# A transformer-like block on one core: cross queries and six of eight convolution columns by seven half-size products, computed ahead of the heads, with results through DRAM

## The chip, the core and the metric

The kernel runs on one core of one Trainium2 chip. A core has TensorE (PE, matrix products; its weight loads are a track of their own, PEld), VectorE (DVE), ScalarE (ACT), GpSimd (POOL) and SyncE (SP, which here only issues DMAs). TensorE writes its results to PSUM, and VectorE and ScalarE read them from there. Each engine works through its own instructions in a fixed order and waits at semaphores for the others. The metric is the device time of one execution in microseconds; less is better.

## What is computed

One layer for 1024 tokens of 1024 channels, in float32, and 256 memory tokens. Cut to what matters:

```python
h = rms_norm(x, g_mix)
c_h, c_b, c_c, sq, sk, sv, xq, gate_pre = split(h @ w_in)     # 1024 columns each, gates 3072
y_conv = (c_b * causal_depthwise_conv(c_c * c_h, conv_w)) @ w_conv_out     # width 3
y_sb   = stick_breaking_attention(sq, sk, sv) @ w_sb_out                   # 16 heads of 64
y_x    = memory_cross_attention(xq, rms_norm(mem), w_mem_kv, ...) @ w_x_out  # 4 heads of 256
g      = sigmoid(gate_pre)
x = x + (g0 * y_conv + g1 * y_sb + g2 * y_x) @ w_out
h2 = rms_norm(x, g_mlp)
x = x + square(relu(h2 @ w_up)) @ w_down
```

Each head of the cross attention normalises its queries and keys, so the queries need a sum of squares over 256 channels.

## The kernel before

**Precision.** Every operand of a matrix product is held as two parts, high and low, each in a reduced format; ScalarE rounds the high part and VectorE subtracts it from the source for the low one (split_w, split; L88 to L118). A product of two such operands is three matmuls: high by high, high by low, low by high (mm3, mm3_steps). A weight tile of 128 x 1024 is loaded by SP into one of 4 buffers (rawp) and split into one of 3 double buffers (whlp) or into two pages. A page is 128 x 1024 floats of SBUF; there are 40, and nearly everything lives in them. The Tile framework gives buffers out, sets the waits and may move an instruction ahead of others on its engine; where the code says keep_in_program_order, the instructions so marked stay in written order among themselves.

**A column of w_in** means 128 of its output channels. project_steps (L211) computes one for 512 tokens: 8 k-tiles by 3 matmuls of 128 x 128 by 128 x 512, 24 in all, yielding twice, so that it can be used as filler: 12 matmuls a step.

**The order of the work.**
1. The start (L316 to L382): memory rows are normalised and transposed; kv(0) to kv(7) compute keys and values in eight groups of 48 matmuls with 256 columns (L281); x is normalised and transposed in two halves into the sixteen pages of hT (norm_transpose, L172, split on the way); the queries of cross head 0 (xq_half, L236), whose squares ScalarE takes from PSUM, and the transposed keys (k_transpose, L357) are woven in.
2. The cross heads (L471 to L493): for each head scores, softmax, transposes and values for two halves of the tokens. Between them run filler steps: for heads 0 to 2 eight steps of the next head's queries, for head 3 the first steps of the values for the other attention (v_steps, L445). Then the rest of the values, whose results go to DRAM, and queries and keys of head pair 0 (sb_qk, L498).
3. The attention heads (L676 to L721): eight pairs, eight query blocks each for two heads. TensorE's scores, ScalarE's sigmoids, POOL's masks, VectorE's scan and product, transposes, splits and the values, two and three steps behind. Filler steps are the gates' columns, the next pair's sb_qk, and in the last pair convolution column 0.
4. Convolution columns 1 to 7 (L722, conv_steps at L625): three products per column, their product with the three taps by ScalarE and VectorE (L644, L646), results split into pages. After that the outputs of the three branches are multiplied by their matrices and gates and merged (L730 to L753), and w_out follows.
5. The MLP's up-projection (L892 to L1036) already uses seven products: the product of a 2 x 2 block matrix by a 2 x 2 block matrix (two columns by two halves of k; two halves of k by two halves of the tokens) needs seven half-size products instead of eight. The operands are sums and differences of blocks (S1 to S4 of the weights, T1 to T4 of the activations, h2_second_a and h2_second_b), and the partial results are accumulated in two PSUM banks and a few SBUF tiles. One unit of two columns is 7 x 12 = 84 matmuls where the plain way takes 96. The order of one unit's products is p1, p2, p6, p5, p7, p3, p4; p1, p6, p7 and p4 accumulate in one bank, and ScalarE copies the state of that bank out after p1 and after p6. All of its vector work is kept in written order.
6. The down-projection, in the same way, and the output.

Of the kernel before, what the change touches and what calls it, by code (L numbers as in the profile page):

```python
# [16 lines left out]
P = 128  # L17
# [25 lines left out]
def block_kernel(ctx, tc, x, mem, small, w_in, w_v, w_kv, w_co, w_so, w_xo, w_out, w_up, w_dn, out):  # L43
# [118 lines left out]
    hT = [None] * KT  # L162

# [47 lines left out]
    def project_steps(w, th, done, cuts=2):  # L211

        ps = pd()
        yield from mm3_steps(
            ps, [(cut(w, k * P, (k + 1) * P), cut(hT[k], th * 512, th * 512 + 512)) for k in range(KT)], cuts
        )
        done(ps)
# [8 lines left out]
    def x_dst(th):  # L226
        def dst(k):
            if hT[k] is None:
                hT[k] = (page(), page())
            return cut(hT[k], th * 512, th * 512 + 512)  # L230

        return dst

    xq_w = {}

    def xq_half(h, st, d2, th, cuts=2):  # L236

        if th == 0:
            if (h, d2) not in xq_w:
                xq_w[h, d2] = unit(w_in[CT_XQ + 2 * h + d2])  # L240
            st["q"][d2] = (page(), page())
            st["sq"][d2] = page(F32)

        def done(ps):
            s = slice(th * 512, th * 512 + 512)
            nc.scalar.activation(st["sq"][d2][:, s], ps, AF.Square)
            q = st["q"][d2]
            split(ps, q[0][:, s], q[1][:, s], scale=sm[:, C_GQ + d2 : C_GQ + d2 + 1])
            if d2 == 1:
                sq = st["sq"]  # L250
                nc.gpsimd.tensor_tensor(out=sq[0][:, s], in0=sq[0][:, s], in1=sq[1][:, s], op=ALU.add)

        yield from project_steps(xq_w[h, d2], th, done, cuts)

    def xq_scale(st):

        sq = st["sq"]
        pss = pt()
        for t in range(8):
            nc.tensor.matmul(  # L260
                pss[:, t : t + 1], lhsT=sq[0][:, t * P : (t + 1) * P], rhs=ones, start=True, stop=True
            )
        r = rstd(pss[:, 0:8], 8, 256)
        st["sc"], st["nsc"] = stat(8), stat(8)
        nc.vector.tensor_scalar_mul(st["sc"], r, 1.0 / 16.0)
        nc.vector.tensor_scalar_mul(st["nsc"], r, -1.0 / 16.0)

    def xq_new():
        return {"q": [None, None], "sq": [None, None]}
# [6 lines left out]
    def kv_split(cg):  # L276
        if cg not in kv_w:
            kv_load(cg)
        kv_w[cg] = [halves(r, True) for r in kv_w[cg]]

    def kv(cg):  # L281

        us = kv_w.pop(cg)
        for i in range(NM):
# [10 lines left out]
            if cg < 4:  # L295
                nc.scalar.copy(kn[i][:, c0 : c0 + 256], ps)
            else:
                split(ps, vx[i][0][:, c0 : c0 + 256], vx[i][1][:, c0 : c0 + 256])

    def k_norm(i):  # L300
# [10 lines left out]
        for h in range(NXH):  # L311
            nc.vector.tensor_scalar_mul(
                kn[i][:, h * 256 : h * 256 + 256], kn[i][:, h * 256 : h * 256 + 256], r[:, h : h + 1]
            )

# [13 lines left out]
    rows0 = [normed(t) for t in xrows]  # L329
    run(kv(1))  # L330
    xq_raw = [load(w_in[CT_XQ + d2]) for d2 in range(2)]
    xrows = load_rows(x, 512, 4)
    kv_split(2)
    kv2 = kv(2)
    for k, _ in enumerate(norm_transpose(rows0, x_dst(0), C_GMIX)):
        fill(kv2, 1)
        if k in (2, 5):
            xq_w[0, k // 3] = halves(xq_raw[k // 3])
    run(kv2)
    st0 = xq_new()  # L340
    run(xq_half(0, st0, 0, 0))
    kv_split(3)
    rows1 = [normed(t) for t in xrows]
    run(xq_half(0, st0, 1, 0))
    kv_split(4)
    weave(norm_transpose(rows1, x_dst(1), C_GMIX), kv(3))
    vx = [(page(), page()) for _ in range(NM)]
    kv_split(5)
    run(kv(4))
    for i in range(NM):  # L350
        k_norm(i)
    run(xq_half(0, st0, 0, 1))
    kv_split(6)
    run(kv(5))
    kx_t = [(page(), page()) for _ in range(2)]

# [16 lines left out]
    def kx(h, d2):  # L373
        dt_ = 2 * h + d2
        return cut(kx_t[dt_ // 4], (dt_ % 4) * M, (dt_ % 4 + 1) * M)

    weave(k_transpose(), xq_half(0, st0, 1, 1, 8))
    kv_split(7)
    run(kv(6))
    xq_scale(st0)  # L380
    run(kv(7))
    pin[0] = False  # L382


    o_scr = [
        [dram.tile([P, 1024], F32, name=f"oscr_{b}_{k}") for k in range(KT)] for b in range(2)
    ]
    g_scr = [
        [dram.tile([P, 1024], F32, name=f"gscr_{b}_{k}") for k in range(KT)] for b in range(3)
    ]  # L390
    v_scr = [dram.tile([P, 4, 1024], F32, name=f"vscr_{c}") for c in range(2)]

# [52 lines left out]
    def v_steps():  # L445

        us = [unit(w_v[0, kp], True) for kp in range(4)]
        for cg in range(2):
            un = []
            for j in range(8):  # L450
                if cg == 0 and j >= 4:
# [6 lines left out]
                            cut(hT[k], j * P, (j + 1) * P),  # L458
# [11 lines left out]

    vgen = v_steps()  # L471
    for h in range(NXH):
        if h + 1 < NXH:
            st1 = xq_new()
            more = chain(*(xq_half(h + 1, st1, d2, th) for d2 in range(2) for th in range(2)))
        else:
            st1, more = None, vgen
        p0 = x_scores(h, st0, 0)
        fill(more, 2)
        p1 = x_scores(h, st0, 1)  # L480
        fill(more, 2)
# [6 lines left out]
        if st1:  # L488
            run(more)
            xq_scale(st1)  # L490
# [272 lines left out]
    }  # L763

# [406 lines left out]
```

## Time and profile before

| | |
|---|---|
| median of 3 runs | 2244.83 us (2242.71 to 2245.02) |
| profiled execution, its own time | 2243.7 us |
| its span in the profile | 2242.0 us |
| TensorE busy | 2187.6 us, 98% of the span, 10304 matmuls |
| VectorE, ScalarE, POOL busy | 58%, 42%, 16% |
| mean granted TensorE clock | 0.994 |
| moved by DMA | 241.91 MB, mean 108 GB/s |

The profile's times are microseconds from the start of the span. A row of the windows gives, for a stretch of the span, its length and the busy time and number of instructions of PE, PEld, DVE, ACT and POOL, then the granted TensorE clock (1 is full speed), the DMA engines' busy share and GB/s. A row of the timeline gives start, duration, engine, line of the code, operation, output and input by the program's names (d, z, t and o are PSUM banks, pg a page, whl a split weight, raw a loaded one), shapes, a count where alike instructions are merged, and in brackets how long the engine sat idle before it and what ended that. A row of the groups gives busy time, the mean ns of one instruction and the idle time before.

### The profile page before, as it was taken

The page shows a single profiled execution, that of the slowest core. Times are in us where ns is not written, and L with a number is a line of the kernel's source. Part 1 is how long each engine was busy: PE and PEld are TensorE (multiplying, and loading weights), DVE is VectorE, ACT ScalarE, POOL GpSimd, SP SyncE. Part 2 cuts the span into 40 slices and gives each one's busy share as a digit, 9 for nine tenths or more (in the row PEclk, how much of TensorE's full clock was granted, in tenths as well). Part 3 has the DMA queues.
Part 4 walks back from the last instruction along what each step waited for, and adds up shares of the span by engine and source line. Part 5 has one row for each costly group of instructions (what it writes and reads, how often), then busy time and mean ns, then how long its engine had stood idle before and what let it go on. Part 6 is the DMA issues. An engine that isn't in the chain of part 4 may idle for free.

```text
span 2242.0 us, 27020 instructions
## 1 busy us (share of the span) xinstructions
PE 2187.6 (98%) x10304; PEld 1817.1 (81%) x10304; DVE 1310.4 (58%) x1781; ACT 948.3 (42%) x1726; POOL 367.4 (16%) x550
## 2 busy tenths in 40 slices
PE   7999999999999999999999999999889999999999
PEld 7988888878878878888888888888678888788887
DVE  5633218787787787773332334442565655777776
ACT  6544316565565665652221121121555555433332
POOL 1011103333333333320000000000111222100000
PEclk9999999999999999999999999999899999999999
DMA  6311322122222222211111344233134444754444
GB/s 226 104 57 59 122 74 85 66 79 82 68 82 77 72 79 76 76 48 57 48 48 47 122 150 150 96 138 114 52 127 155 155 155 150 271 174 141 141 153 139
DMA packets 68786, 241.91 MB, mean 108 GB/s; under 512 B 9008, under 2 KB 9008, under 8 KB 68656
## 3 DMA queue, kind: packets, MB, share of 16 engines
q1 hardware_dynamic: 50224, 177.26, 24.5%
q0 software_dynamic: 18432, 62.93, 7.6%
q8 instruction: 81, 1.33, 0.3%
q14 instruction: 49, 0.40, 0.1%
HBM read 168.85 MB, written 62.91 MB: 103 GB/s over the span
## 4 chain that ended last, share of the span: by engine, by line
PE 80%; DVE 7%; ACT 4%; issue 4%; POOL 3%; DMA 0%; POOLq 0%; DVEq 0%; ACTq 0%; SPq 0%
PE d L205 12%; PE d L207 12%; PE d L206 12%; PE d L810 4%; PE d L806 4%; PE d L125 4%; PE d L127 4%; PE d L809 4%; PE d L126 4%; PE z L806 3%; PE z L809 3%; PE z L810 3%; POOL pg L558 2%; PE o L597 2%; DVE pg L114 1%
## 5 line engine op out<-in xcount | busy, mean ns | idle before, releaser
L205 PE MATMUL d<-pg,whl 128*128 128x512 f32 x1152 | 456.4, 396 | 0.0
L207 PE MATMUL d<-pg,whl 128*128 128x512 f32 x1152 | 449.9, 390 | 0.0
L206 PE MATMUL d<-pg,whl 128*128 128x512 f32 x1152 | 449.7, 390 | 0.0
L777 ACT ACTIVATE pg<-pg 128x512 f32<-128x512 f32 (+2 forms) x180 | 140.2, 782 | 295.9 <-DVE pg L774 293.9
L207 PEld LDWEIGHTS d<-pg,whl 128*128 128x128 f32 x1152 | 216.2, 188 | 47.0
L205 PEld LDWEIGHTS d<-pg,whl 128*128 128x128 f32 x1152 | 216.5, 188 | 40.9
L206 PEld LDWEIGHTS d<-pg,whl 128*128 128x128 f32 x1152 | 216.6, 188 | 40.5
L558 POOL TENSOR_SCALAR_AFFINE_SELECT pg<-pg 128x128 f32<-128x128 f32 x256 | 168.0, 663 | 304.8 <-ACT pg L555 291.8
L568 DVE TENSOR_TENSOR_SCAN pg<-pg,zero 128x128 f32<-128x128 f32 (+7 forms) x128 | 177.3, 1385 | 57.5 <-POOL pg L558 55.0
L90 DVE TENSOR_TENSOR whl<-raw,whl 128x1024 fp32r<-128x1024 f32 x96 | 121.7, 1268 | 152.4 <-ACT whl L89 151.6
L113 ACT CAST pg<-t 128x256 fp32r<-128x256 f32 (+2 forms) x336 | 115.2, 368 | 203.9 <-DVE pg L114 141.5
L89 ACT CAST whl<-raw 128x1024 fp32r<-128x1024 f32 x96 | 101.5, 1058 | 228.4 <-PE d L207 82.6
L774 DVE TENSOR_TENSOR pg<-pg,pg 128x1024 fp32r<-128x1024 f32 (+3 forms) x144 | 149.6, 1043 | 64.4 <-ACT pg L777 63.1
L114 DVE TENSOR_TENSOR pg<-t,pg 128x256 fp32r<-128x256 f32 (+2 forms) x336 | 129.3, 404 | 65.6 <-ACT pg L113 62.1
L125 PE MATMUL d<-pg,whl 128*128 128x512 f32 x384 | 149.4, 389 | 0.0
L126 PE MATMUL d<-pg,whl 128*128 128x512 f32 x384 | 149.4, 389 | 0.0
L127 PE MATMUL d<-pg,whl 128*128 128x512 f32 x384 | 149.4, 389 | 0.0
L205 PE MATMUL d<-pg,pg 128*128 128x512 f32 (+1 forms) x384 | 138.9, 362 | 0.4 <-ACT pg L116 0.4
L206 PE MATMUL d<-pg,pg 128*128 128x512 f32 (+1 forms) x384 | 137.9, 360 | 0.5 <-DVE pg L90 0.5
L207 PE MATMUL d<-pg,pg 128*128 128x512 f32 (+1 forms) x384 | 137.9, 360 | 0.0
L806 PE MATMUL d<-pg,whl 128*128 128x512 f32 x288 | 115.3, 401 | 11.8 <-ACT whl L777 7.7
L809 PE MATMUL d<-pg,whl 128*128 128x512 f32 x288 | 114.8, 398 | 1.2 <-DVE pg L774 1.2
(180 smaller groups left out, 4176.3 us busy)
## 6 DMA issues: line engine op xcount, KB each, us to landing
raw<-in_w_in SPq DMA_DIRECT2D x72, 512.0 KB, 3.6
raw<-in_w_up SPq DMA_DIRECT2D x32, 512.0 KB, 4.0
raw<-fscr_s SPq DMA_DIRECT2D x32, 512.0 KB, 4.0
pg<-in_w_dn SPq DMA_DIRECT2D x32, 512.0 KB, 5.1
gscr<-pg POOLq DMA_DIRECT2D x24, 512.0 KB, 2.9
raw<-gscr SPq DMA_DIRECT2D x24, 512.0 KB, 3.3
fscr<-pg POOLq DMA_DIRECT2D x48, 256.0 KB, 3.3
fscr_s<-pg POOLq DMA_DIRECT2D x48, 256.0 KB, 2.9
```

The source lines that it names most:

```text
L114: nc.vector.tensor_tensor(out=lo, in0=src, in1=f32v(hi), op=ALU.subtract)
L125: nc.tensor.matmul(ps, lhsT=ah, rhs=bh, start=i == 0, stop=False)
L126: nc.tensor.matmul(ps, lhsT=ah, rhs=bl, start=False, stop=False)
L127: nc.tensor.matmul(ps, lhsT=al, rhs=bh, start=False, stop=i == n - 1)
L205: nc.tensor.matmul(ps, lhsT=ah, rhs=bh, start=i == 0, stop=False)
L206: nc.tensor.matmul(ps, lhsT=ah, rhs=bl, start=False, stop=False)
L207: nc.tensor.matmul(ps, lhsT=al, rhs=bh, start=False, stop=i == n - 1)
L558: nc.gpsimd.affine_select(out=t_[:, W - P : W], in_=t_[:, W - P : W], pattern=[[-1, P]], compare_op=ALU.is_gt, fill=fill_, base=0, channel ...
L568: nc.vector.tensor_tensor_scan(out=rev, data0=rev, data1=zero.broadcast_to([P, W]), initial=1.0, op0=ALU.mult, op1=ALU.add)
L806: m_ = nc.tensor.matmul(ps, lhsT=ah, rhs=bh, start=first and i == 0, stop=False, **go)
L809: nc.tensor.matmul(ps, lhsT=ah, rhs=bl, start=False, stop=False, **go)
L810: nc.tensor.matmul(ps, lhsT=al, rhs=bh, start=False, stop=i == n - 1, **go)
```

## The change

The seven-product unit is made general and used twice more. Seconds holds the activations' halves and their sums and differences for a normalised x, Unit the seven products of one pair of columns, drive the order of a list of units (the old order of the MLP's units, with the list extra put between the first products). Four units make the cross queries (one per head); nine make convolution columns 2 to 7: for each pair of columns one unit for the h part, one for the C part, one for the B part. They run right after the start and before the cross heads. Their results go to DRAM by POOL's queue: raw queries to q_scr, finished convolution columns to u_scr. Column 0 stays filler of the last head pair, column 1 becomes filler of the cross heads, together with sb_qk of pair 0.

```diff
+    class Seconds:
...
+        def first(self, rows):
+            for kk in range(4):
+                raw = self.raw[kk] = pair()
+                for j in range(2):
+                    self.tile(rows, kk + 4 * j, raw[:, j, :])
+                    yield
+                hi, lo = pair(F32R), pair(F32R)
+                split(flat(raw), flat(hi), flat(lo))
...
+        def second_a(self, rows, kk):
+
+            r0, r1, ta = self.raw[kk], pair(), pair()
+            for j in range(2):
+                self.tile(rows, kk + 4 * j, r1[:, j, :])
+            if self.keep:
+                nc.gpsimd.dma_start(out=self.keep[kk // 2][:, kk % 2, :], in_=r1[:, 0, :])
+            vec(ta[:, 0, :], r1[:, 0, :], ALU.subtract, r0[:, 0, :])
+            vec(ta[:, 1, :], r1[:, 1, :], ALU.subtract, ta[:, 0, :])
+            self.h["t1"][kk], self.h["t2"][kk] = split_pair(ta)
+            vec(r0[:, 0, :], r1[:, 1, :], ALU.subtract, r1[:, 0, :])
+            vec(r0[:, 1, :], r0[:, 1, :], ALU.subtract, ta[:, 1, :])
+            self.new[kk] = r1
...
+            if u < 2:
+                un.w4()
+            else:
+                un.p1()
+                U[u - 1].fin()
+                un.w3()
+                un.p2()
+                un.w4()
+            if u + 2 < NU:
+                U[u + 2].load()
+            if u >= 2:
+                un.p6()
+                un.p5()
+            if u >= 1 and nx:
+                nx.w1()
+            un.p7()
+            if u == 0:
+                nx.w3()
+            elif nx:
+                nx.w2()
+            un.p3()
+            un.p4()
```

The first stages in their new order. kv's results for the values and the normalised keys go to DRAM and come back later; the queries and the key transposes leave this stage:

```diff
+    weave(sec_h.first(rows0), kv(2))
     kv_split(3)
+    kv_load(4)
     rows1 = [normed(t) for t in xrows]
...
+    run(kv(3))
+    kv_load(5)
     for i in range(NM):
         k_norm(i)
...
+    for kk in range(4):
+        kv_split(4 + kk)
+        steps = kv(4 + kk)
+        fill(steps, 4)
+        if kk + 6 < 8:
+            kv_load(kk + 6)
+        sec_h.second_a(rows1, kk)
+        run(steps)
+    for i in range(NM):
+        nc.gpsimd.dma_start(out=kv_scr[1][i], in_=vr[i])
```

The new units. fin of a unit is called in the unit after it, behind that one's p1; act and vec keep the written order, and so do the taps here:

```diff
+    class CUnit(Unit):
...
+        def fin(self):
+            self.cv = []
+            for i in range(2):
+                prod = flat(self.tiles[i])
+                vec(prod, prod, ALU.mult, flat(self.hu.tiles[i]))
+                cv = flat(self.hu.tiles[i])
+                taps(self.c0 + i, prod, cv, act, lambda **kw: order(nc.vector.scalar_tensor_tensor(**kw)))
+                self.cv.append(cv)
...
+    class BUnit(Unit):
...
+        def fin(self):
+            for i in range(2):
+                b = flat(self.tiles[i])
+                vec(b, b, ALU.mult, self.cu.cv[i])
+                nc.gpsimd.dma_start(out=u_scr[self.c0 + i], in_=b)
...
+    units = [QUnit(h) for h in range(NXH)]
+    for c in range(2, KT, 2):
+        hu = HUnit(c)
+        cu = CUnit(c, hu)
+        units += [hu, cu, BUnit(c, cu)]
+    drive(units, [lambda kk=kk: sec_h.second_b(kk) for kk in range(4)])
+
+
+    h12 = [load(t.rearrange("p a b -> p (a b)")) for t in h12_scr]
+    kn = [page(F32) for _ in range(NM)]
+    for i in range(NM):
+        nc.sync.dma_start(out=kn[i], in_=kv_scr[0][i])
+    for kk in range(4):
...
+        split_o(h12[kk // 2][:, j * 512 : j * 512 + 512], *sec_h.h["12"][kk])
```

The values and the cross heads. Queries are loaded, squared and split from SBUF (xq_load, xq_split), and a head has five filler steps of 12 matmuls:

```diff
+    vgen = v_steps()
+    fill(vgen, 17)
+    st0 = xq_load(0)
+    vr = [load(kv_scr[1][i]) for i in range(NM)]
+    weave(k_transpose(), vgen)
+    vx = [halves(r, True) for r in vr]
+    xq_split(st0)
+    more = chain(sb_qk(0, nxt), conv_steps(1))
+    fill(more, 1)
+    xq_scale(st0)
+    st1 = None
+    for h in range(NXH):
+        if h + 1 < NXH:
+            st1 = xq_load(h + 1)
+        p0 = x_scores(h, st0, 0)
+        fill(more, 1)
+        p1 = x_scores(h, st0, 1)
+        fill(more, 1)
+        t0 = x_transpose(p0)
+        fill(more, 1)
+        x_values(h, 0, t0)
+        if h + 1 < NXH:
+            xq_split(st1)
+        fill(more, 1)
+        t1 = x_transpose(p1)
+        fill(more, 1)
+        if h + 1 < NXH:
+            xq_scale(st1)
+        x_values(h, 1, t1)
+        st0 = st1
+    run(more)
```

In the last pair the finished columns come back, and the loop over columns 1 to 7 is gone:

```diff
+                if p == NPAIR - 1 and hd == 1 and i in (3, 5, 6, 7):
+                    u.append(unit(u_scr[1 + len(u)], True))
...
+    while len(u) < KT - 1:
+        u.append(unit(u_scr[1 + len(u)], True))
     run(more)
-    for c in range(1, KT):
-        run(conv_steps(c))
+    u = u0 + u
```

The MLP's units become a subclass of Unit with the same instructions in the same order.

546 lines of the change are left out of this document (253 added, 293 removed).

## The prediction

> **What bounds the kernel now.** I read the page first: engine totals, the chain that ended last, the groups.
>
> ```profile
> PE 2187.6 (98%) x10304; PEld 1817.1 (81%) x10304; DVE 1310.4 (58%) x1781; ACT 948.3 (42%) x1726; POOL 367.4 (16%) x550
> PE 80%; DVE 7%; ACT 4%; issue 4%; POOL 3%; DMA 0%; POOLq 0%; DVEq 0%; ACTq 0%; SPq 0%
> L205 PE MATMUL d<-pg,whl 128*128 128x512 f32 x1152 | 456.4, 396 | 0.0
> ```
>
> TensorE is busy nearly always and carries 80% of the chain. So a removed matmul counts, but its price is not the 396 ns of its row. In the timeline of TensorE the starts show the price:
>
> ```profile
> 20.04 0.28 PE L207 MATMUL d<-pg,pg 128*128 128x256 f32 x1
> 20.16 0.28 PE L205 MATMUL d<-pg,pg 128*128 128x256 f32 x1
> 1652.23 0.39 PE L806 MATMUL d<-pg,whl 128*128 128x512 f32 x1
> 1652.46 0.39 PE L809 MATMUL d<-pg,whl 128*128 128x512 f32 x1
> 1607.56 1.03 PE L819 MATMUL t<-ident,pg 128*128 128x128 f32 x8
> 1608.35 0.48 PE L806 MATMUL d<-pg,whl 128*128 128x512 f32 x1
> ```
>
> Busy times overlap: a 512-column matmul starts 0.23 us after the last one, a 256-column one 0.12 us, eight transposes take 0.79 us. Now the windows, cut where the stages end:
>
> ```profile
> 0.00:100.70 100.70, 87.79 (x592) 80.27 (x593) 60.48 (x100) 61.95 (x113) 12.46 (x21) 0.98 0.53 183
> 100.70:240.00 139.30, 138.46 (x756) 119.28 (x755) 51.76 (x125) 58.06 (x130) 23.77 (x26) 1.00 0.16 57
> 240.00:334.20 94.20, 94.17 (x416) 77.66 (x415) 14.14 (x15) 19.63 (x29) 10.36 (x15) 1.00 0.32 101
> 334.20:1011.40 677.20, 659.95 (x3242) 545.32 (x3242) 530.50 (x760) 400.15 (x935) 246.02 (x350) 1.00 0.23 74
> 1011.40:1240.00 228.60, 228.60 (x1011) 189.28 (x1010) 72.29 (x78) 45.53 (x57) 1.30 (x2) 1.00 0.15 49
> 1680.00:1736.00 56.00, 56.00 (x249) 46.37 (x248) 33.68 (x45) 29.61 (x44) 11.27 (x21) 1.00 0.47 155
> ```
>
> They are: the start (memory keys and values, normalised x, head 0's queries); the cross heads; the rest of the values and pair 0; the attention heads; the conv columns 1 to 7; a stretch of the MLP's up-projection, which already uses seven products. The conv stage is 7 x 144 = 1008 matmuls in 228.6 us, 0.2268 us each with no gap. The up stretch is as dense, so a seven-product unit in full swing costs its matmuls alone: 84 x 0.2268 = 19.05 us, where the plain way takes 96.
>
> **Part 1, products.** Removed: 8 query columns (384 matmuls) and 6 conv columns (864), 1248 in all, 283.0 us. Added: 13 units of 84, 1092, 247.7 us. Gain 35.4 us. The group's mean of 390 to 396 ns would have made it 61. [...]
>
> Everything after 1240.0 us is the same work in the same order, so I forecast the new time of that mark, stage by stage.
>
> **Part 2, the start.** Its present 100.7 us hold 384 kv matmuls (46.1 us), 96 query matmuls (21.8) and 96 transposes (9.5): 77 us of work, 23 of loss. Up to 26.6 us nothing changes. The queries and the key transposes leave, and with them TensorE's cover for the vector work; the second half's tiles get differences and splits (second_a) instead of one split. Its rows, from the MLP's entry, and those of splits:
>
> ```profile
> 26.64 1.13 PE L178 MATMUL t<-ident,pg 128*128 128x128 f32 x6
> 1600.67 1.48 DVE L774 TENSOR_TENSOR pg<-pg,pg 128x512 f32<-128x512 f32 x2
> 1603.28 1.23 DVE L774 TENSOR_TENSOR pg<-pg,pg 128x1024 fp32r<-128x1024 f32 x1 [1.12 <-ACT pg L777]
> 1605.02 2.08 DVE L774 TENSOR_TENSOR pg<-pg,pg 128x512 f32<-128x512 f32 x3
> 1608.23 1.23 DVE L774 TENSOR_TENSOR pg<-pg,pg 128x1024 fp32r<-128x1024 f32 x1 [1.12 <-ACT pg L777]
> 27.11 2.00 ACT L89 CAST pg<-raw 128x1024 fp32r<-128x1024 f32 x2
> 68.41 2.35 DVE L90 TENSOR_TENSOR pg<-raw,pg 128x1024 fp32r<-128x1024 f32 x2
> ```
>
> One second_a holds VectorE for 1608.23 - 1603.28 = 4.95 us, its own wait for ScalarE included; a kv group's two splits add 2.3. Four rounds make 29 us, against 4 x (5.8 + 0.8) = 26 us on TensorE: VectorE paces this loop. It begins after first() with kv(2), paced by ScalarE (from 29.1 us eight tile copies of 0.6, four splits of 1.0 and evictions: about 39) and after kv(3) (5.8 us and a wait for its split: 46), with the norms of rows 4 to 7 and the key norms in the way of ScalarE: at 47 to 50. The loop then ends at 76 to 79. I take **79**, the late end, since a gap of 2 to 4 us ahead of kv(4) may halve the clock once. Bounds: 71 (TensorE's own work from 39) and 86 (two half-clock spells and 2 us more).
>
> **Part 3, the units.** The prologue has second_b alone. Up to w2 of unit 1, VectorE has two w1 (2.4 us), four second_b (1.9 each), two sums (0.7) and two w2 (3.6 each, rows below): about 18 us, some of it ahead of the first product, where TensorE has six products, 16 us: 1 us lost (0 to 5). Q and H units are lighter than the up units (no relu, no sums). The C units are not. Their fin (product and taps, all in written order) is issued in the B unit that follows, between p1's copy and w3. Rows for it:
>
> ```profile
> 1604.14 0.60 ACT L777 ACTIVATE xh<-d 128x512 f32<-128x512 f32 x1 [0.90 <-PE d L810]
> 998.83 1.15 ACT L644 ACTIVATE pg<-pg,sm 128x1024 f32<-128x1024 f32 x1 [1.65 <-DVE pg L637]
> 1000.78 2.59 DVE L646 SCALAR_TENSOR_TENSOR pg<-pg,sm,pg 128x1023 f32<-128x1023 f32 x2
> 1654.32 1.22 DVE L774 TENSOR_TENSOR whl<-raw,whl 128x1024 fp32r<-128x1024 f32 x1
> 1636.65 0.69 DVE L774 TENSOR_TENSOR pg<-raw,raw 128x512 f32<-128x512 f32 x1
> 1637.97 1.06 ACT L777 ACTIVATE whl<-pg 128x1024 fp32r<-128x1024 f32 x1 [2.10 <-DVE pg L774]
> 1639.06 1.22 DVE L774 TENSOR_TENSOR whl<-pg,whl 128x1024 fp32r<-128x1024 f32 x1 [1.12 <-ACT whl L777]
> ```
>
> Clock from the start of B's p1. p1 ends at 2.9; ScalarE copies it to 3.5, and only then may start the first tap, to 4.6. VectorE adds two taps to 7.2, then multiplies the second column (1.2) to 8.3; ScalarE's second tap to 9.5; two more on VectorE to 12.1. Now w3: two subtractions to 13.3, ScalarE's high part to 14.4, w4's high part to 14.9, and behind it in ScalarE's order the copy of p6, to 15.5. p7 continues in p6's bank and needs that copy, and w3's weights. TensorE is there after p1, p2, p6, p5 = 48 x 0.2268 = 10.9 us. So it waits **4.6 us** in each of three B units. What such a wait does to the clock:
>
> ```profile
> 1598.54 0.69 PE L819 MATMUL t<-ident,pg 128*128 128x128 f32 x2 [3.99 <-DVE pg L159]
> 1600.74 0.63 PE L809 MATMUL d<-pg,whl 128*128 128x512 f32 x1
> 1601.16 0.63 PE L810 MATMUL d<-pg,whl 128*128 128x512 f32 x1
> 1603.71 0.39 PE L810 MATMUL d<-pg,whl 128*128 128x512 f32 x1
> 1622.64 0.79 PE L806 MATMUL d<-pg,whl 128*128 128x512 f32 x1 [2.96 <-ACT pg L777]
> 1627.78 0.40 PE L809 MATMUL z<-pg,whl 128*128 128x512 f32 x1
> 1639.08 0.80 PE L806 MATMUL d<-pg,whl 128*128 128x512 f32 x1 [4.42 <-ACT whl L777]
> 1644.72 0.39 PE L806 MATMUL z<-pg,whl 128*128 128x512 f32 x1
> ```
>
> After each of these gaps matmuls start 0.42 us apart for 5.1 to 5.6 us, not 0.23: some 2.4 us more. The Trainium skill (TensorE: Matmul & The Clock Gate, What's actually happening) gives a warm-up of about 3.4 us at half rate. By that figure, as an estimate, the addition would be 1.7 us and the three units would cost 19 us, not 21; the trace differs with its 5.1 to 5.6 us and decides. So 3 x (4.6 + 2.4) = **21 us** (0 if the gaps close, 27 if w3 comes 2 us later still).
>
> **Part 4, values and cross heads.** Now 334.2 - 100.7 = 233.5 us. Out go the query fills of three heads (288 matmuls, 65.3 us); in come conv column 1 (144, 32.7 us) and 16 key transposes (1.6 us): 202.5. Two edges are new. First, the saved half h12 is split in written order after the last B unit's fin: two multiplies (2.0 us after the last product) and four half splits, 4.4 us; the last two value weights wait for its load buffers.
>
> ```profile
> raw<-in_w_in SPq DMA_DIRECT2D x72, 512.0 KB, 3.6
> ```
>
> They land at 8 us and are split by 10.6. TensorE meanwhile has the first four k of three value tiles (36 matmuls, 8.2 us) and the key transposes if the scheduler takes them ahead, as it interleaves chains at the start: 1.5 us (0 to 9). On the SP queue the loads of the keys and of w_v stand behind h12's; all land in a stretch with 16% DMA. Second, a head has 5 fills of 12 matmuls, 13.6 us, where three heads had 8. From a half's scores to its transposes lie 8.3 us of other TensorE work (one fill, the other half's scores, another fill).
>
> ```profile
> 102.37 0.69 DVE L408 TENSOR_REDUCE st<-z 128x2 f32<-128x512 f32 x1 [0.61 <-PE z L127]
> 103.91 0.56 ACT L413 ACTIVATE pg<-z,st,st 128x256 f32<-128x256 f32 x1
> ```
>
> One tile's softmax is through its exponentials 2.1 us after its maximum began; two tiles with their scaling need some 5, so the fills still cover it: 2 us for small gaps (0 to 20, rival 2). SP's query loads are issued a head ahead of their split, POOL's addition two fills ahead of xq_scale.
>
> **Part 5, heads and after.** 677.2 us as before. Column 1 to 7's results come back as seven loads and splits in the last pair, in place of 228.6 us of conv. The last three splits (2.3 us each) compete for pages with the last head's tiles, and the first merge needs all eight columns in its first chain: 2.5 us (0 to 8). The transfers added are 10.5 MB out by POOL's queue, which has nothing else in the units' stage, and 10.5 MB back by SP's; I cost them at nothing, as the windows' DMA shares are 0.15 to 0.5 outside the start; without that cover a late one costs 3.6 us.
>
> **Sum.** 79 + 247.7 + 1 + 21 + 202.5 + 1.5 + 2 + 677.2 + 2.5 = 1234.4 against 1240.0: 5.6 us earlier. The profiled execution took 2243.7 us (span 2242.0), the median is 2244.83, 1.1 more. So 2238.1 on that run and 2239 on the median; I write **2238**. The 35 us are real and 27 of them go to waits.
>
> **Rivals.**
> 1. The B units do not wait, because the scheduler puts the taps elsewhere or VectorE catches up. For: the up stage, same skeleton, has no gap. Against: the order is written out, and no up unit has 10 us between p1's copy and w3. Gain 21 more: 2217.
> 2. Slower: pages in the cross-head loop. There are 40. x halves 16, keys 4, values 4, pair 0's six, one head's queries 4 and squares 2, two softmax tiles, a transposed pair of 2 make 40, and conv column 1 wants two more. If the next head's query splits wait for pages until x_values has freed them, scores start late: about 5 us and a half-clock spell, 7.4, in three heads, 22 us: 2260. It decides from (6 + 4.5)/3 = 3.5 us per head on. Against: the fixed order places those splits just where the old queries die.
> 3. The vector work of the new units paces all 13 (1.5 us each, 20 us): 2258. Against: VectorE's 33.68 of 56 us in the up stretch.
>
> **How the numbers follow.** Forecast 0.50 (own range 2230 to 2247), rival 1 0.24, rival 2 0.19, rival 3 and others 0.07. A difference under 0.2% (4.5 us: 2240.3 to 2249.3) cannot be told from none. Of the forecast's 0.50, two thirds lie below 2240.3: faster 0.33 + 0.24 = 0.57; same 0.20; slower 0.23. Range 2213 (rival 1 with a quicker start) to 2257.
>
> **What would show it.** Seven-product units 19.05 us long; three gaps of 4 to 5 us on TensorE in B units before p7, each with a granted clock of 0.5 behind it; first product near 79 us; heads' stage starting near 555 us and 677 long; merge starting near 1234. Wrong if those gaps are absent, if the start runs past 86, or if gaps of over 3 us per head stand in the cross heads.

## The result, and the profile after

The changed kernel takes 2268.78 us (median of 4 runs, 2268.47 to 2269.87), the kernel before 2244.93 beside it. It is slower by 24 us, outside the range of 2213 to 2257. The ratio given with the result is 1.0113, its 95% interval 1.0101 to 1.0126 (the two medians alone give 1.0106). The profiled execution took 2269.87 us; its span is 2268.1, 26.1 more than the span before. One execution in what follows was disturbed, the profiled one of run 5 (4315 us), so that run has a time but no marks. First the page of the changed kernel: the totals, the chain, and the group of the products' first line.

```profile
PE 2174.7 (96%) x10148; PEld 1800.8 (79%) x10148; DVE 1406.0 (62%) x1885; ACT 1004.3 (44%) x1791; POOL 385.1 (17%) x570
PE 71%; DVE 10%; issue 7%; ACT 7%; POOL 4%; DMA 1%; POOLq 0%; DVEq 0%; ACTq 0%; SPq 0%
L265 PE MATMUL d<-pg,whl 128*128 128x512 f32 x444 | 179.6, 404 | 29.3 <-ACT pg L236 17.7
```

The work did go: 156 matmuls fewer, and TensorE 13 us less busy. But TensorE's part of the chain fell from 80% to 71%, and VectorE's, ScalarE's and the issue of instructions rose by 3 points each. The last row names one line, the first of a product's three (the MLP's units have it too): 29.3 us of idle time ahead of it, 17.7 of it ended by ScalarE. The windows, cut at the ends of the new stages (start, units, values and cross heads, attention heads):

```profile
0.00:93.90 93.90, 67.48 (x464) 63.17 (x464) 53.00 (x82) 58.35 (x103) 12.84 (x26) 0.91 0.54 196
93.90:370.80 276.90, 259.10 (x1100) 210.95 (x1100) 147.90 (x175) 87.63 (x119) 6.92 (x13) 0.96 0.24 79
370.80:579.30 208.50, 203.55 (x1035) 172.22 (x1036) 85.22 (x158) 87.64 (x165) 36.95 (x40) 0.98 0.36 117
579.30:1266.50 687.20, 665.18 (x3263) 548.97 (x3261) 538.16 (x770) 408.19 (x946) 253.49 (x354) 1.00 0.24 77
```

The merge's first product lies at 1266.53. In the kernel before, it lies at 1241.48; these are TensorE's first product of the conv columns and the merge's first product there:

```profile
1012.98 0.40 PE L205 MATMUL d<-pg,whl 128*128 128x512 f32 x1
1241.48 0.39 PE L125 MATMUL d<-pg,whl 128*128 128x512 f32 x1
```

So 25.1 of the 26.1 us are lost ahead of the merge, and what comes behind takes 1 us more than before. (The prediction's marks, 1011.40 and 1240.0, are both about 1.5 us early. Its stages add up all the same, but by its own terms the heads' stage is 678.8 us long and the forecast for the merge 1236.0, not 677.2 and 1234.4.) The clock column shows where to look, 0.91, 0.96 and 0.98 in the first three stages. In the timeline of TensorE these are the main gaps behind it (in brackets the idle time and what ended it):

```profile
45.54 0.58 PE L204 MATMUL d<-whl,pg 128*128 128x256 f32 x1 [4.14 <-DVE whl L90]
59.53 0.58 PE L204 MATMUL d<-whl,pg 128*128 128x256 f32 x1 [3.10 <-DVE whl L90]
77.03 0.50 PE L203 MATMUL d<-whl,pg 128*128 128x256 f32 x2 [0.54 <-ACT whl L89]
85.48 0.50 PE L203 MATMUL d<-whl,pg 128*128 128x256 f32 x2 [0.53 <-ACT whl L89]
93.92 0.50 PE L265 MATMUL d<-pg,whl 128*128 128x512 f32 x1 [1.42 <-ACT whl L236]
121.59 0.61 PE L269 MATMUL d<-pg,whl 128*128 128x512 f32 x1 [0.53 <-DVE whl L233]
230.91 0.69 PE L265 MATMUL d<-pg,whl 128*128 128x512 f32 x1 [4.52 <-ACT pg L236]
294.48 0.79 PE L265 MATMUL d<-pg,whl 128*128 128x512 f32 x1 [4.52 <-ACT pg L236]
358.71 0.79 PE L265 MATMUL d<-pg,whl 128*128 128x512 f32 x1 [4.53 <-ACT pg L236]
373.43 0.96 PE L203 MATMUL d<-pg,pg 128*128 128x512 f32 x3 [2.82 <-ACT pg L89]
1266.53 0.79 PE L125 MATMUL d<-pg,whl 128*128 128x512 f32 x1 [3.05 <-ACT whl L89]
```

Five places: key and value groups 3 and 4 and the rounds after them, which are 8.45 us apart (85.48 - 77.03) where 7.25 were expected; the first units; three B units, each 4.5 us late at p7; the first value products; the first merge product. The first unit's product is at 93.92, not 79.

The B units go as the prediction had them step by step. These are ScalarE's rows of the first, whose p1 began at 215.35:

```profile
218.27 0.60 ACT L236 ACTIVATE xh<-d 128x512 f32<-128x512 f32 x1 [2.12 <-PE d L269]
218.76 1.14 ACT L236 ACTIVATE pg<-pg,sm 128x1024 f32<-128x1024 f32 x1
223.78 1.15 ACT L236 ACTIVATE pg<-pg,sm 128x1024 f32<-128x1024 f32 x1 [3.87 <-DVE pg L233]
228.80 1.06 ACT L236 ACTIVATE whl<-pg 128x1024 fp32r<-128x1024 f32 x1 [3.87 <-DVE pg L233]
230.28 0.58 ACT L236 ACTIVATE pg<-d 128x512 f32<-128x512 f32 x1
```

The copy of p1, the first tap, the second tap, w3's high part, and the copy of p6 that p7 waits for: forecast to end at 15.5 us on p1's clock, measured at 230.28 + 0.58 = 230.86, which is 215.35 + 15.5.

### The profile page after: what moved, and what is told of

Its sections match the earlier page's. It is cut to its first block, busy times and chain, and to the rows that moved or that the text cites. A ratio compares the mean times of both kernels' runs of the same rounds, so it can differ in the third digit from the quotient of the medians.

```text
span 2268.1 us, 27004 instructions
## 1 busy us (share of the span) xinstructions
PE 2174.7 (96%) x10148; PEld 1800.8 (79%) x10148; DVE 1406.0 (62%) x1885; ACT 1004.3 (44%) x1791; POOL 385.1 (17%) x570
## 3 DMA queue, kind: packets, MB, share of 16 engines
q0 software_dynamic: 21504, 73.94, 8.7%
## 4 chain that ended last, share of the span: by engine, by line
PE 71%; DVE 10%; issue 7%; ACT 7%; POOL 4%; DMA 1%; POOLq 0%; DVEq 0%; ACTq 0%; SPq 0%
PE d L204 7%; PE d L205 6%; PE d L203 6%; PE d L269 6%; PE d L265 6%; PE d L268 6%; PE d L125 4%; PE d L126 4%; PE d L127 4%; PE z L265 4%; PE z L269 4%; PE z L268 4%; POOL pg L836 3%; DVE pg L233 2%; DVE pg L114 2%
## 5 line engine op out<-in xcount | busy, mean ns | idle before, releaser
L203 PE MATMUL d<-pg,whl 128*128 128x512 f32 x736 | 294.6, 400 | 0.3 <-ACT ox L744 0.3
L204 PE MATMUL d<-pg,whl 128*128 128x512 f32 x736 | 288.0, 391 | 0.0
L205 PE MATMUL d<-pg,whl 128*128 128x512 f32 x736 | 287.8, 391 | 0.0
L236 ACT ACTIVATE pg<-pg 128x512 f32<-128x512 f32 (+1 forms) x192 | 150.9, 791 | 305.6 <-DVE pg L233 303.6
L233 DVE TENSOR_TENSOR pg<-pg,pg 128x1024 fp32r<-128x1024 f32 (+3 forms) x180 | 184.7, 1032 | 72.2 <-ACT pg L236 70.4
L265 PE MATMUL d<-pg,whl 128*128 128x512 f32 x444 | 179.6, 404 | 29.3 <-ACT pg L236 17.7
L269 PE MATMUL d<-pg,whl 128*128 128x512 f32 x444 | 178.8, 403 | 2.5 <-DVE whl L233 2.4
L268 PE MATMUL d<-pg,whl 128*128 128x512 f32 x444 | 178.4, 402 | 1.2 <-DVE pg L233 1.2
L205 PEld LDWEIGHTS d<-pg,whl 128*128 128x128 f32 x736 | 138.2, 188 | 30.7
L203 PEld LDWEIGHTS d<-pg,whl 128*128 128x128 f32 x736 | 138.4, 188 | 25.8 <-ACT ox L744 1.1
L204 PEld LDWEIGHTS d<-pg,whl 128*128 128x128 f32 x736 | 138.6, 188 | 24.4
L265 PE MATMUL z<-pg,whl 128*128 128x512 f32 x396 | 154.9, 391 | 0.0
L269 PE MATMUL z<-pg,whl 128*128 128x512 f32 x396 | 154.6, 390 | 0.0
L268 PE MATMUL z<-pg,whl 128*128 128x512 f32 x396 | 154.6, 390 | 0.0
L125 PE MATMUL d<-pg,whl 128*128 128x512 f32 x384 | 150.7, 393 | 3.0 <-ACT whl L89 3.0
L89 ACT CAST whl<-raw 128x1024 fp32r<-128x1024 f32 x78 | 82.6, 1059 | 158.7 <-DMA raw<-in_w_co 62.8
L126 PE MATMUL d<-pg,whl 128*128 128x512 f32 x384 | 150.5, 392 | 0.0
L127 PE MATMUL d<-pg,whl 128*128 128x512 f32 x384 | 149.9, 391 | 0.0
L114 DVE TENSOR_TENSOR pg<-t,pg 128x256 fp32r<-128x256 f32 (+2 forms) x336 | 129.3, 404 | 30.5 <-ACT pg L113 27.1
```

The source lines that it names most:

```text
L125: nc.tensor.matmul(ps, lhsT=ah, rhs=bh, start=i == 0, stop=False)
L126: nc.tensor.matmul(ps, lhsT=ah, rhs=bl, start=False, stop=False)
L127: nc.tensor.matmul(ps, lhsT=al, rhs=bh, start=False, stop=i == n - 1)
L203: nc.tensor.matmul(ps, lhsT=ah, rhs=bh, start=i == 0, stop=False)
L204: nc.tensor.matmul(ps, lhsT=ah, rhs=bl, start=False, stop=False)
L205: nc.tensor.matmul(ps, lhsT=al, rhs=bh, start=False, stop=i == n - 1)
```

## The experiments

Theory, formed from the trace: the products save what they should, and the time goes to separate stalls, each made by the written order of ScalarE and VectorE (work that could run stands behind work that waits for TensorE). The rival for the start is what the prediction had: VectorE has too much to do there. For the rest the rival is that a stall removed only shows the next one. Times are medians, and what a run saves is counted from the changed kernel's 2268.78. The kernel before took 2244.9 us beside the changed kernel, 2242.1 us beside the first four runs, 2242.7 beside the next four and 2241.9 beside the last three.

**1. Splits of the value groups written ahead.**

```diff
+    kv_split(4)
     for kk in range(4):
-        kv_split(4 + kk)
...
+        if kk < 3:
+            kv_split(5 + kk)
         run(steps)
```

> One part of the changed start is altered: the split of the next kv group is written ahead of the second half of the present kv group (and the first of them ahead of the key norms), nothing else. Theory A (order): in the changed kernel the split of group n+1 stands on ScalarE behind the copy of group n's second result, so that each round is the sum of split, 48 matmuls and copy, 8.45 us; with the split ahead VectorE's own work paces a round, 7.2 us, and the gaps of 0.5 and 0.8 us before each group on TensorE go. First seven-product unit at 82 to 86 us in place of 93.9, time 8 to 12 us less: 2257 to 2261. Rival B (VectorE paces the loop already, or the halved clock does it): rounds stay at 8.4 us, time within 3 us of 2268.8.

Measured 2267.21 us (ratio 1.0111, 1.0096 to 1.0126). VectorE's rows:

```profile
57.13 1.14 DVE L513 TENSOR_SCALAR pg<-pg,st 128x256 f32<-128x256 f32 x4 [1.14 <-POOL st L150]
60.40 1.14 DVE L513 TENSOR_SCALAR pg<-pg,st 128x256 f32<-128x256 f32 x4 [2.05 <-POOL st L150]
61.45 1.48 DVE L233 TENSOR_TENSOR pg<-pg,pg 128x512 f32<-128x512 f32 x2
66.40 1.22 DVE L90 TENSOR_TENSOR whl<-raw,whl 128x1024 fp32r<-128x1024 f32 x1
73.62 1.22 DVE L90 TENSOR_TENSOR whl<-raw,whl 128x1024 fp32r<-128x1024 f32 x1
```

The rounds are now 7.2 us apart (73.62 - 66.40), so the order does set the period. But the loop's first subtraction still comes at 61.45, behind the key norms and their two waits for POOL, and the first product moves only from 93.9 to 90.8. Of these 3.1 us, 1.9 are there at group 3's gap already (43.63 against 45.54), ahead of the edit; profiles of the same start differ by that much (runs 4 and 7, which leave the start alone, are 1.5 and 1.3 us early there). The time, 1.6 us less, falls within rival B's 3 us though the rounds went theory A's way: the size that theory A gave was wrong, as the larger part of the loss is ahead of the loop.

**2. VectorE relieved in the same loop.**

```diff
-            vec(ta[:, 0, :], r1[:, 0, :], ALU.subtract, r0[:, 0, :])
-            vec(ta[:, 1, :], r1[:, 1, :], ALU.subtract, ta[:, 0, :])
-            self.h["t1"][kk], self.h["t2"][kk] = split_pair(ta)
-            vec(r0[:, 0, :], r1[:, 1, :], ALU.subtract, r1[:, 0, :])
-            vec(r0[:, 1, :], r0[:, 1, :], ALU.subtract, ta[:, 1, :])
+            if not self.keep:
+                vec(ta[:, 0, :], r1[:, 0, :], ALU.subtract, r0[:, 0, :])
+                vec(ta[:, 1, :], r1[:, 1, :], ALU.subtract, ta[:, 0, :])
+            self.h["t1"][kk], self.h["t2"][kk] = split_pair(r1 if self.keep else ta)
...
```

> The four differences of second_a in the new stage are left out (the sums T1 to T4 there are not formed, so queries and convolution columns are not the reference's); VectorE has 2.6 us less work in each of four rounds. Theory A (order): the rounds stay at 8.4 us or lose at most 0.6, time 2266 to 2269. Rival B (VectorE's work paces the loop, as the prediction had it): rounds of 5.9 us, 10 us less, 2258.

Measured 2270.83 us (1.0126, 1.0111 to 1.0141). TensorE's rows at the starts of two rounds:

```profile
77.33 0.50 PE L203 MATMUL d<-whl,pg 128*128 128x256 f32 x2 [0.54 <-ACT whl L89]
85.78 0.50 PE L203 MATMUL d<-whl,pg 128*128 128x256 f32 x2 [0.54 <-ACT whl L89]
```

Still 8.45 us, with four subtractions less in each round. In the changed kernel VectorE's load does not pace this loop. What does is one chain over three engines, in its own rows of ScalarE and VectorE:

```profile
75.66 0.37 ACT L499 COPY pg<-d 128x256 f32<-128x256 f32 x1 [1.98 <-PE d L205]
75.93 1.05 ACT L89 CAST whl<-raw 128x1024 fp32r<-128x1024 f32 x1
```

```profile
77.01 1.23 DVE L90 TENSOR_TENSOR whl<-raw,whl 128x1024 fp32r<-128x1024 f32 x1 [1.12 <-ACT whl L89]
```

The next group's split (L89) has its data, and stands behind the copy of this group's last result (L499), which waits for TensorE; TensorE then waits for the split. That the split could have run earlier is what run 1 shows.

**3. Conv sums split around w3.** Column 0's product and taps stand ahead of p4 in the C unit, column 1's product ahead of w3 and its taps behind it; but every unit's sums, the MLP's too, moved behind w3 with them.

```diff
-                U[u - 1].fin()
+                U[u - 1].mid()
                 un.w3()
+                U[u - 1].fin()
...
             un.p3()
+            un.early()
             un.p4()
```

> The same taps and products of the C units, but column 0's are written ahead of p4, column 1's product ahead of the B unit's w3 and its taps behind that w3. Theory C (written order): the three gaps of 4.52 us ahead of p7 in the B units and the halved clock behind them go; 17 to 21 us less, 2248 to 2252. Rival D (the B units have too much vector work for 19 us, so that the wait moves to a later product): at most 8 us less, 2261 or more, with gaps ahead of p4 or of the next unit's p1.

Measured 2255.23 us (1.0059, 1.0044 to 1.0074), 13.5 us less: neither theory's size. The three gaps at p7 are gone, and with them their half clock. The first value product and the first merge product, in TensorE's timeline:

```profile
352.51 0.96 PE L203 MATMUL d<-pg,pg 128*128 128x512 f32 x3 [2.46 <-ACT pg L89]
1246.19 0.80 PE L125 MATMUL d<-pg,whl 128*128 128x512 f32 x1 [3.38 <-ACT whl L89]
```

The first is 20.9 us earlier than 373.43, the second 20.3 us earlier than 1266.53, but the time is only 13.5 us less: some 7 us are lost again behind the merge.

**4. Taps without the written order.** They are still issued at the same place, but the scheduler may move them.

```diff
-                taps(self.c0 + i, prod, cv, act, lambda **kw: order(nc.vector.scalar_tensor_tensor(**kw)))
+                taps(self.c0 + i, prod, cv, nc.scalar.activation, nc.vector.scalar_tensor_tensor)
```

> The taps of the C units are no longer held in written order; the framework then puts ScalarE's first tap ahead of the copy of p1 and leaves the rest. Theory C: each gap shrinks from 4.5 to some 2.0 us and the halved clock mostly stays away: 12 to 16 us less, 2253 to 2257. Rival D: under 6 us.

Measured 2258.77 us (1.0074, 1.0057 to 1.0091), 10.0 us less where theory C gave 12 to 16. The gaps shrink to 2.20, 2.20 and 2.19 us, but the halved clock stays behind two of the three (last section). Rival 1 of the prediction, that the scheduler would close the gaps, is half true where it is allowed to act.

**5. As 3, but for the conv units alone.** The sums of the other units stay where they were; late() issues column 1's taps behind w3.

```diff
                 U[u - 1].fin()
                 un.w3()
+                U[u - 1].late()
```

> Only the conv units are changed here: column 0's product and taps ahead of p4, column 1's product ahead of w3, column 1's taps behind w3; the sums of the other units stay where they were. Theory A (the three gaps before p7 with the half clock behind them cost about 20 us, and nothing else is lost by the move): first value product near 352.5, first merge product near 1246, and that lead of 20 us kept to the end: 2248 to 2251. Rival B (part of the lead is given back behind the merge whatever is done, because the merge's stores or loads pace it): the mark at 1246, the end at 2254 to 2257, as with all sums moved.

Measured 2248.73 us (1.0025, 1.0016 to 1.0035), 20 us less than the changed kernel. By its time theory A holds, though without marks: the 7 us lost in run 3 came from moving the other units' sums, the only difference between the two.

**6. The start's splits ahead.** Group 3 is split ahead of the interleaved first rows, groups 4 to 7 as in run 1, and the key norms move behind the loop.

```diff
+    kv_split(3)
     weave(sec_h.first(rows0), kv(2))
-    kv_split(3)
...
-    for i in range(NM):
-        k_norm(i)
-    del kn
+    kv_split(4)
...
+    for i in range(NM):
+        k_norm(i)
+    del kn
```

> Memory key and value group 3 is split ahead of the interleaved first rows, group 4 ahead of the loop, groups 5 to 7 ahead of their round's first copy, and the key norms move behind the loop. Theory A (the start is late because splits stand in ScalarE's and VectorE's written order behind copies and norms that wait for TensorE): gaps at group 3 go, rounds of 7 us or less, first product of the units at 77 to 82 instead of 93.9, the time 12 to 17 us less, 2252 to 2257. Rival B (the start is bound by VectorE's own work, which is only moved about): the first product stays later than 88, the time within 6 us of 2268.8.

Measured 2264.01 us (1.0093, 1.0078 to 1.0108). Of A's 12 to 17 us only 4.8 came, within B's 6, though the first product stands at 82.73, close to A's mark. TensorE's rows and VectorE's show why that mark deceives:

```profile
82.73 0.50 PE L265 MATMUL d<-pg,whl 128*128 128x512 f32 x1 [3.01 <-ACT whl L236]
87.52 0.80 PE L269 MATMUL d<-pg,whl 128*128 128x512 f32 x1 [4.06 <-DVE whl L233]
```

```profile
82.06 1.14 DVE L513 TENSOR_SCALAR pg<-pg,st 128x256 f32<-128x256 f32 x4 [2.00 <-POOL st L150]
85.19 1.14 DVE L513 TENSOR_SCALAR pg<-pg,st 128x256 f32<-128x256 f32 x4 [1.91 <-POOL st L150]
```

Two matmuls start early, the third waits 4.06 us: the key norms, moved, now stand ahead of the first unit's weights on VectorE.

**7. The two edges' buffers.**

```diff
-    h12 = [load(t.rearrange("p a b -> p (a b)")) for t in h12_scr]
+    h12 = [page(F32) for _ in h12_scr]
...
+    w_first = unit(w_co[0])
```

> The saved half h12 is loaded into pages instead of the raw load buffers, and the first merge weight is loaded and split ahead of the last columns' results. Theory A (both edges wait for load buffers that written-ahead splits hold): the 2.8 and 0.8 us gaps at the first value product and the 3.05 us gap at the first merge product go, with the half clock behind each: 3 to 5 us at each mark, 2259 to 2264 in all. Rival B (pages run short at the values, or the last column's split and not the weight ends the merge's wait): the gaps stay or move, within 2 us of 2268.8.

Measured 2263.46 us (1.0092, 1.0077 to 1.0107). The two edges answer differently:

```profile
372.93 0.96 PE L203 MATMUL d<-pg,pg 128*128 128x512 f32 x3 [2.82 <-ACT pg L89]
1261.49 0.39 PE L125 MATMUL d<-pg,whl 128*128 128x512 f32 x1
```

At the merge the gap is gone and the first product 5.0 us earlier, as theory A has it. What was late there, in the changed kernel, is the weight's load: SP issues it only at 1261.57, and ScalarE's split waits for it:

```profile
1265.43 1.04 ACT L89 CAST whl<-raw 128x1024 fp32r<-128x1024 f32 x1 [0.69 <-DMA raw<-in_w_co]
```

The edit moves load and split together, so it does not tell a held load buffer from mere order. At the values theory A falls: the same 2.82 us, so load buffers are not what the split waits for.

**8. Runs 5, 6 and 7 together.**

> The three edits of the runs beside it together: conv sums split around w3, splits of the start written ahead, the two edges' buffers. Theory A (the losses are separate stalls at separate places, so they add): the sum of the three savings, about 20 + 14 + 9 = 43 us, 2222 to 2235, below the kernel before. Rival B (a stall removed lets the next limit show, so that they add to less): 2240 or more, no faster than the kernel before.

Measured 2234.35 us (0.9963, 0.9950 to 0.9975), faster than the kernel before. The three savings (20.1, 4.8 and 5.3) add to 30.1; together they bring 34.4, within theory A's range and not B's, though two of its three terms were too large. At the merge's first product the leads add to 33.2 (with run 3's in place of run 5's) against 33.5.

**9. The key norms out of the start.** As run 6, but the squares stand in query units 1 and 2 ahead of p4, the scaling behind the next unit's w3.

```diff
-    for i in range(NM):
-        k_norm(i)
-    del kn
...
+        def early(self):
+            if 1 <= self.head <= NM:
+                k_stats(self.head - 1)
+        def late(self):
+            if 1 <= self.head <= NM:
+                k_scale(self.head - 1)
```

> As the run with the splits of the start written ahead (first product at 82.7, then a 4.05 us wait for VectorE, 2264.0 us), but the key norms stand in the query units 1 and 2, not ahead of the first units: squares ahead of p4, scaling behind the next unit's w3. Theory A (what keeps the start late once the splits are ahead is the key norms, whose two round trips to GpSimd hold VectorE for 6 us ahead of the first unit's weights): the 4 us gap goes, the first product lies at 79 to 81, the mark of unit 2's start 5 to 8 us earlier than in that run, 2256 to 2260. Rival B (VectorE has no room left, another of its steps takes the place): within 2 us of 2264.

Measured 2256.45 us (1.0065, 1.0051 to 1.0078), 7.6 less than run 6. TensorE's first product, and VectorE's splits:

```profile
80.98 0.51 PE L265 MATMUL d<-pg,whl 128*128 128x512 f32 x1 [1.42 <-ACT whl L236]
```

```profile
65.29 1.22 DVE L90 TENSOR_TENSOR whl<-raw,whl 128x1024 fp32r<-128x1024 f32 x1
72.51 1.22 DVE L90 TENSOR_TENSOR whl<-raw,whl 128x1024 fp32r<-128x1024 f32 x1
```

The 4 us gap is gone. The loop's first split stands at 49.71 and the next at 56.93, 65.29 and 72.51: two of the three rounds take 7.22 us, as in run 1, and that is the prediction's VectorE pace (4.95 + 2.3); the other takes 8.36, with a wait of 1.04 us for ScalarE.

**10. The first value weights ahead of h12.** They are loaded in the unit before the last, and split behind the last p7.

```diff
+            if u + 2 == NU and ahead:
+                ahead()
...
             elif nx:
                 nx.w2()
+            elif last:
+                last()
...
-        us = [unit(w_v[0, kp], True) for kp in range(4)]
+        us = v_w + [unit(w_v[0, kp], True) for kp in range(2, 4)]
```

> The changed kernel with one edit at the values' edge: the first two value weights are loaded ahead of the last conv unit's end and split behind its p7, ahead of the four half splits of h12. Theory A (the 2.8 and 0.8 us gaps there come from the written order: the weights' splits stand on ScalarE and VectorE behind h12's, which stand behind the last copy): both gaps and the half clock behind them go, 4 to 7 us at the first value product and as much at the end, 2262 to 2265. Rival B (something else, pages or the load, is late next): less than 2 us.

Measured 2262.67 us (1.0089, 1.0074 to 1.0105), and the values begin without a gap:

```profile
369.56 0.39 PE L203 MATMUL d<-pg,pg 128*128 128x512 f32 x1
```

That is 3.9 us earlier; at the merge the lead is 6.7 us (1259.87 against 1266.53), since the half clock behind the gap is gone too. What held the weights' split was h12's four splits in the written order.

**11. All that moved a mark.** Runs 5, 9 and 10 and the merge weight of run 7; h12 goes back to the load buffers.

> All edits that moved a mark: conv sums around w3, the splits of the start ahead, the key norms in the query units, the values' first weights ahead of h12 (which goes back to the load buffers), the first merge weight ahead of the last results. If the stalls are separate, 2234.3 of the three earlier edits together, less 4 to 7 for the norms and 2 to 5 for the values' edge: 2223 to 2229. If they hide one another: 2232 to 2236.

Measured 2225.35 us (0.9924, 0.9912 to 0.9936), 16.6 us or 0.76% below the kernel before. From its page and the start of its merge:

```profile
PE 2158.7 (97%) x10148; PEld 1789.7 (80%) x10148; DVE 1404.5 (63%) x1885; ACT 1003.9 (45%) x1791; POOL 383.8 (17%) x570
1222.12 0.39 PE L125 MATMUL d<-pg,whl 128*128 128x512 f32 x1
```

The matmuls are those of the changed kernel, 10148, and so is VectorE's and ScalarE's work within 0.2%. Only its order differs, and one buffer.

Do the stalls add? By medians the parts' savings, 20.1 + 12.3 + 6.1, and 5.3 for run 7, make 43.8, and 43.4 are measured. That they agree so well is in part luck: the kernel before was 2 to 3 us slower beside the changed kernel than beside the later runs. With each run set against the kernel before of its own batch, the parts make 33 and the whole 40. At the merge's first product the leads of the parts are 20.3 (run 3 in place of run 5), 14.9, 6.7 and 5.0 (runs 9, 10 and 7), together 46.9, and the whole leads by 44.4. In no reckoning does the whole fall short of its parts by more than 2.5 us, so these stalls do not hide one another.

## Why the prediction was wrong

With its marks put right it gave 1236.0 us for the merge's first product; the trace shows 1266.5. By stages the 30.5 us are: start 14.9 (93.9 against 79), units 7.2 (276.9 against 247.7 + 1 + 21), values and cross heads 2.5 (208.5 against 206.0), heads and the merge's entry 5.9 (687.2 against 681.3). Two smaller slips are in its sums: of the 35.4 us, 29.8 and not 27 go to waits when 5.6 are left as the gain, and the transfers added are 11.0 MB each way by the two pages (POOL's queue 73.94 against 62.93), not 10.5. And its range, up to 2257, left out both slower outcomes that it named itself, 2260 and 2258. By its steps:

- **Products: right.** 35.4 us of TensorE's work went, at 0.2268 us for a matmul, not at 0.39. With most of the stalls away, run 11 has 19 us of them in the mark of the merge (1241.5 to 1222.1).
- **The waits in B units: right.** 4.6 us forecast, 4.52 measured, three times. From p1 to the next unit's p1 (the last one to its end) the three take 25.5, 26.1 and 26.4 us instead of 19.05, 20.9 in all where 21 were forecast, and run 3 won back 20.3 at the merge. The clock's part of it, 2.4 us each, is right only on average (last section).
- **The start: wrong, 14.9 us** (79 forecast, 93.9 measured, beyond even the late bound of 86). The step that failed is "VectorE paces this loop", begun "at 47 to 50". It was a sum of VectorE's work, and the sum was right (7.25 us a round; run 9 shows 7.22). What it missed is that a split on ScalarE stands behind a copy that waits for TensorE, which makes rounds of 8.45 us, and that VectorE comes to the loop only after the row norms' and key norms' round trips to POOL. VectorE's rows of the last key norm and the loop's first split:

```profile
57.20 1.14 DVE L513 TENSOR_SCALAR pg<-pg,st 128x256 f32<-128x256 f32 x4 [2.05 <-POOL st L150]
58.26 1.22 DVE L90 TENSOR_TENSOR whl<-raw,whl 128x1024 fp32r<-128x1024 f32 x1
```

The loop begins at 58.26 instead of 50 at the latest, 8.26 us, and from there to the first product at 93.92 the four rounds take 35.66 us instead of 29, 6.66 more. The gaps of 4.1 and 3.1 us ahead of groups 3 and 4 each brought a spell of half clock (granted 0.67 from 40 to 50 us and 0.66 from 55 to 65); the sum had allowed for one. Run 1 shows the rounds, runs 6 and 9 the gaps and the norms. With all that away the loop begins at 49.7 and the first product comes at 81.0 (run 9), close to the forecast; but the forecast had the key norms in the start, and that start no longer has them.

- **The prologue of the units: 1 us forecast (0 to 5), 7.2 measured.** Unit 2 begins at 139.19; two dense units after 93.92 would end at 132.0:

```profile
139.19 0.39 PE L265 MATMUL d<-pg,whl 128*128 128x512 f32 x1
```

There are gaps of 0.5 to 1.6 us at 95.2, 112.2, 113.4, 120.3 and 121.6 and a spell of half clock behind the last. No run tried this; run 11 still has it, with 8.6 us. VectorE is busy for 15.7 of the 19.5 us from 93.9 to 113.4, so load and order can't be told apart here.

- **The values' edge: 1.5 forecast, 6.7 measured** (run 10). The prediction named the last two value weights, as waiting for h12's load buffers; late were the first two, which stand behind the same splits in the written order, and run 7 shows that the buffers don't matter. The rest of this stage came out 2.7 us below its sum; 0.8 us of that are eight key transposes that ran ahead of the cut at 370.8, and no run separates the rest.
- **The merge's entry: 2.5 forecast; 4.5 measured at the mark** (run 7: 5.0 earlier, 0.5 of it there already at the values), and a spell of half clock behind it. The column splits were named, not what they delay: the merge's first weight is loaded and split behind them, and doing both ahead ends the wait.
- **Rival 2, pages in the cross heads: not seen.** The largest gap there is 0.75 us. Its direction, slower, came true for another reason. Rival 3, VectorE's pace in all units, is not seen either: from 130 to 210 us TensorE is busy without a gap.
- **Left open:** some 4 us in the attention heads, forecast as unchanged: the stage is 8.4 us longer than the 678.8 before, and the merge's entry explains 4.5 of it. No run separates the rest.

So the error was not in the cost of the work but in the edges between stages. They were costed by an engine's load; at the start and at the values the engine's order decided, at the merge's entry a load and a split that came late, and at the units' prologue the cause stays open.

## What to carry to other kernels

Where the busiest engine has next to no slack, ask at each new edge not how much work the other engines have, but what stands ahead of the instruction that the busy engine needs next, and what that waits for in its turn. Splits and loads of the next step belong ahead of the copies and norms of this one; a norm with a round trip to another engine belongs where a long run of products covers it. If a change saves real work and loses time, look for the stalls one by one: here none hid another, and mending the order turned 24 us lost into 17 won.

## What the hardware showed besides

The price of a gap for the clock is not the same each time. Two windows of 12 us, each around one of the 4.5 us gaps at p7 in the changed kernel (the third number from the end is the granted clock):

```profile
225.00:237.00 12.00, 7.48 (x27) 5.63 (x26) 8.77 (x11) 3.49 (x5) 0.00 (x0) 0.86 0.27 87
290.00:302.00 12.00, 7.52 (x23) 5.97 (x24) 7.96 (x10) 3.67 (x6) 0.00 (x0) 0.72 0.25 87
```

0.86 is 3.4 us at half clock ((1 - 0.86) x 12 / 0.5), 0.72 is 6.7 us. In half-microsecond windows the first spell begins with the products, at 231, and ends at 234.4; the second begins inside the gap, at 292.5, and ends at 299.3. So the same gap costs the products behind it 3.4 or 4.8 us at half rate, in the third unit some 5.5, where the prediction took 5.1 to 5.6 throughout. The Trainium skill (TensorE: Matmul & The Clock Gate, What's actually happening) gives a warm-up of about 3.4 us; these spells are one and two times that.

Shorter gaps can cost as well. In run 4, behind the first of the three gaps of 2.2 us, no spell shows; behind the second, TensorE's matmuls first start 0.23 us apart and only a microsecond later 0.43:

```profile
287.41 0.40 PE L268 MATMUL d<-pg,whl 128*128 128x512 f32 x1
287.65 0.40 PE L269 MATMUL d<-pg,whl 128*128 128x512 f32 x1
...
288.52 0.63 PE L269 MATMUL d<-pg,whl 128*128 128x512 f32 x1
288.95 0.63 PE L265 MATMUL d<-pg,whl 128*128 128x512 f32 x1
```
